# PEER stage: routing, weighing and the u-projection as one software pipeline with a kept order, and one of four one-hot products moved to ScalarE

## The chip, the cores and the metric

The kernel runs on one core of a Trainium2 chip. The metric is device time in microseconds (us) of one execution; a figure for a kernel is the median of its runs. One profiled execution gives the trace from which all rows here come. Engines carry the trace's names: PE is TensorE (PEld its weight loads), DVE VectorE, ACT ScalarE, POOL GpSimd, SP the engine that issues the loads.

## The reference, cut to what matters

The network has two blocks of two layers each on 256 tokens of width 1024. The change lies in the feed-forward part of the first block (PEER), which is run once in each of its two layers:

```python
def peer_ffn(h, w_q, sub_keys, u, v):          # u, v: 16384 experts x 1024
    q = (xc @ w_q).reshape(-1, 8, 2, 64)        # 8 heads, two halves
    s = jnp.einsum('thpd,pkd->thpk', q, sub_keys)
    sv, si = lax.top_k(s, 16)                   # best 16 of 128 keys, each half
    cand = sv[:, :, 0, :, None] + sv[:, :, 1, None, :]
    cand_id = si[:, :, 0, :, None] * 128 + si[:, :, 1, None, :]
    cv, ci = lax.top_k(cand, 16)                # best 16 pairs
    eid = jnp.take_along_axis(cand_id, ci, -1)
    g = softmax(cv)
    a = gelu(jnp.einsum('td,thkd->thk', xc, u[eid]))
    return jnp.einsum('thk,thkd->td', g * a, v[eid])
...
mods = silu(c) @ ada_w + ada_b                  # 12 x 1024 numbers, six vectors per layer
x = x + g1 * mixer(modulate(rms_norm(x), sh1, sc1))
x = x + g2 * peer_ffn(modulate(rms_norm(x), sh2, sc2), ...)
```

## The kernel before, in words

The kernel does not gather experts. It computes gelu(x u) for all 16384 experts in 128 **units** of 128 experts (`up`, lines 664 to 678), multiplies them by a dense weight that is zero where an expert was not chosen, and then accumulates all 128 units against v (`down`, lines 680 to 684).

*A unit of u.* A unit is 128 x 1024 weights, half of a 1 MB load (line 138, SP; two buffers `w_raw`). Every product is made from three: the weights are split into a rounded part `w_hi` (line 155, ACT) and a remainder `w_lo` (line 146, DVE or POOL), three buffers each, and 24 matmuls (lines 183 to 185) give 128 experts by 256 tokens in PSUM. The letters of a pattern say which engine makes `w_lo`: "P" is POOL, "V" is DVE, "VP" takes them in turn. ACT's gelu writes the unit into its place in `ring` (line 673). For tokens whose weights are already in `ring`, it writes to a scratch tile `sq` (line 676) and DVE multiplies that into `ring` (line 677).

*Routing.* After the keys' scores (line 744), DVE finds the top 16 of 128 for 32 rows (`top`, lines 716 to 721: maximum, index, replace, maximum, index), builds 50 candidates (line 756), finds their top 16, turns positions into key numbers (`ra`, lines 771 to 785; `eq`, lines 795 to 803), and makes the softmax (ACT's exp, line 783, between gelus, so ACT loads its function table for it and again afterwards). PE turns the results by six transposes (lines 816 to 818).

*Weighing.* For a block of 4 tokens (64 blocks) DVE builds two one-hot tiles of 128 x 512 (line 826: first key; line 828: second key) and multiplies the second by the high and by the low part of the softmax (line 830, two products, G1 and G2). PE makes 8 matmuls of 128 x 128 from them (lines 833 and 835), which is the dense weight of 128 x 128 experts for 4 tokens. DVE multiplies it into the units that are already done (line 839), and ACT copies it into the places of the units still to come (line 841).

*What sets the order.* Instructions are recorded in the order of the program, which calls `up` some units at a time between the parts of the routing, and two units after every four blocks. A scheduler with a cost model then orders each engine's stream by its own priorities; nothing in this stage pins it. The remaining `ada` blocks (the columns of ada_w that are needed late: 56 loads of 512 KB, line 381 on SP, each followed by a DVE multiply-and-sum of 128 x 1024, line 356) stand in the program in the down stage of PEER, one after every second unit. The scheduler moves them ahead to wherever SP and DVE look free.

## Time and profile before

| | us |
|---|---|
| median of 3 runs (lowest to highest) | 3672.56 (3648.35 to 3685.4) |
| the profiled execution, its time | 3682.53 |
| the profiled execution, its span | 3680.7 |
| mean granted clock of TensorE | 0.955 |
| PEER of layer 0: units of u with routing and weighing | 238 to 777.6 |
| PEER of layer 0: units of v | 777.6 to 1142.3 |
| PEER of layer 1: units of u with routing and weighing | 1381.5 to 1909.5 |
| PEER of layer 1: units of v | 1909.5 to 2274.2 |

The first 238 us hold the start of `ada` and the mixer of layer 0, 1142 to 1381 us the mixer of layer 1; the rest after 2274 us is the second block. PE is busy 94% of the whole span, so what can be gained lies in the stretches in which it isn't. A mean over the span hides those: the views are read stage by stage.

### The profile page before, as it was taken

The page shows a single profiled execution, that of the slowest core. Times are in us where ns is not written, and L with a number is a line of the kernel's source. Part 1 is how long each engine was busy: PE and PEld are TensorE (multiplying, and loading weights), DVE is VectorE, ACT ScalarE, POOL GpSimd, SP SyncE. Part 2 cuts the span into 40 slices and gives each one's busy share as a digit, 9 for nine tenths or more (in the row PEclk, how much of TensorE's full clock was granted, in tenths as well). Part 3 has the DMA queues.
Part 4 walks back from the last instruction along what each step waited for, and adds up shares of the span by engine and source line. Part 5 has one row for each costly group of instructions (what it writes and reads, how often), then busy time and mean ns, then how long its engine had stood idle before and what let it go on. Part 6 is the DMA issues. An engine that isn't in the chain of part 4 may idle for free.

```text
span 3680.7 us, 64031 instructions
## 1 busy us (share of the span) xinstructions
PE 3474.1 (94%) x26071; PEld 3201.5 (87%) x26071; DVE 2485.7 (68%) x4491; ACT 1738.2 (47%) x2934; POOL 1155.0 (31%) x536
## 2 busy tenths in 40 slices
PE   5888898999999998798999999999999999999999
PEld 4578888999998668787999999997769999978799
DVE  7689899877777449699777677555735454656544
ACT  3243444444445444344444445444644454555543
POOL 3165001444444126100444444443024232311422
PEclk9699899999999889899999999999979999999999
DMA  7554523755555113422555555543224555433254
GB/s 264 193 201 166 185 91 134 248 186 184 184 184 189 58 47 127 149 87 86 183 184 183 185 184 194 184 176 137 81 80 162 184 182 180 170 115 115 91 184 149
DMA packets 85848, 576.62 MB, mean 157 GB/s; under 512 B 9855, under 2 KB 11248, under 8 KB 20016
## 3 DMA queue, kind: packets, MB, share of 16 engines
q1 hardware_dynamic: 82448, 567.35, 43.0%
q8 instruction: 204, 3.34, 0.4%
q0 software_dynamic: 1520, 3.30, 0.3%
q10 hardware_dynamic: 1584, 1.88, 0.2%
q14 instruction: 92, 0.75, 0.1%
HBM read 571.54 MB, written 1.34 MB: 156 GB/s over the span
## 4 chain that ended last, share of the span: by engine, by line
PE 76%; DVE 16%; DMA 3%; ACT 2%; issue 2%; POOL 0%; ACTq 0%; SPq 0%; DVEq 0%; POOLq 0%
PE acc L185 13%; PE acc L184 13%; PE acc L183 13%; PE mm L185 8%; PE mm L183 8%; PE mm L184 8%; DVE w_lo L146 3%; DMA ada<-ada 3%; DVE ada L356 1%; PE g L833 1%; PE g L835 1%; DVE ring L839 1%; ACT w_hi L155 1%; PE pv L441 1%; DVE ring L721 1%
## 5 line engine op out<-in xcount | busy, mean ns | idle before, releaser
L146 POOL TENSOR_TENSOR w_lo<-w_raw,w_hi 128x1024 fp32r<-128x1024 f32 x441 | 1084.4, 2462 | 2450.9 <-ACT w_hi L155 2421.1
L155 ACT ACTIVATE w_hi<-w_raw 128x1024 fp32r<-128x1024 f32 x980 | 1037.8, 1060 | 1376.7 <-PE acc L184 676.3
L146 DVE TENSOR_TENSOR w_lo<-w_raw,w_hi 128x1024 fp32r<-128x1024 f32 x539 | 663.9, 1233 | 184.4 <-ACT w_hi L155 173.9
L183 PE MATMUL mm<-xh,w_hi 128*128 128x256 f32 (+1 forms) x2568 | 734.3, 287 | 18.8 <-ACT xh L316 11.1
L185 PE MATMUL mm<-xh,w_lo 128*128 128x256 f32 (+1 forms) x2568 | 738.0, 288 | 13.9 <-DVE w_lo L146 12.0
L184 PE MATMUL mm<-xl,w_hi 128*128 128x256 f32 (+1 forms) x2568 | 736.1, 287 | 4.6 <-DVE xl L317 3.0
L183 PE MATMUL acc<-wh,w_hi 128*128 128x256 f32 x2048 | 575.1, 281 | 0.0
L184 PE MATMUL acc<-wl,w_hi 128*128 128x256 f32 x2048 | 575.1, 281 | 0.0
L185 PE MATMUL acc<-wh,w_lo 128*128 128x256 f32 x2048 | 575.1, 281 | 0.0
L183 PEld LDWEIGHTS mm<-xh,w_hi 128*128 128x128 f32 (+1 forms) x2568 | 491.4, 192 | 33.2 <-issue 17.9
L185 PE MATMUL acc<-xh,w_lo 128*128 128x256 f32 (+1 forms) x1536 | 452.8, 295 | 68.7 <-DVE w_lo L146 65.7
L185 PEld LDWEIGHTS mm<-xh,w_lo 128*128 128x128 f32 (+1 forms) x2568 | 493.0, 192 | 23.0 <-DVE w_lo L146 17.3
L184 PEld LDWEIGHTS mm<-xl,w_hi 128*128 128x128 f32 (+1 forms) x2568 | 491.4, 191 | 13.5 <-issue 4.4
L446 DVE TENSOR_TENSOR wl<-ring,wh 128x256 fp32r<-128x256 f32 x256 | 359.5, 1405 | 185.2 <-ACT wh L445 185.1
L183 PE MATMUL acc<-xh,w_hi 128*128 128x256 f32 (+1 forms) x1536 | 446.1, 292 | 28.4 <-ACT xh L316 22.4
L184 PE MATMUL acc<-xl,w_hi 128*128 128x256 f32 (+1 forms) x1536 | 448.3, 292 | 3.4 <-DVE xl L270 2.7
L184 PEld LDWEIGHTS acc<-wl,w_hi 128*128 128x128 f32 x2048 | 386.3, 189 | 0.0
L183 PEld LDWEIGHTS acc<-wh,w_hi 128*128 128x128 f32 x2048 | 386.3, 189 | 0.0
L185 PEld LDWEIGHTS acc<-wh,w_lo 128*128 128x128 f32 x2048 | 386.3, 189 | 0.0
L185 PEld LDWEIGHTS acc<-xh,w_lo 128*128 128x128 f32 x1536 | 302.9, 197 | 78.3 <-DVE w_lo L146 74.2
L183 PEld LDWEIGHTS acc<-xh,w_hi 128*128 128x128 f32 x1536 | 301.6, 197 | 32.1 <-ACT xh L316 23.8
L184 PEld LDWEIGHTS acc<-xl,w_hi 128*128 128x128 f32 x1536 | 301.3, 196 | 6.6 <-DVE xl L270 3.9
(450 smaller groups left out, 6058.7 us busy)
## 6 DMA issues: line engine op xcount, KB each, us to landing
w_raw<-ffn SPq DMA_DIRECT2D x132, 1024.0 KB, 4.8
w_raw<-peer_u SPq DMA_DIRECT2D x128, 1024.0 KB, 4.8
w_raw<-peer_v SPq DMA_DIRECT2D x128, 1024.0 KB, 4.8
w_raw<-mix_in SPq DMA_DIRECT2D x48, 1024.0 KB, 4.8
ada<-ada SPq DMA_DIRECT2D x56, 512.0 KB, 4.2
w_raw<-mix_out SPq DMA_DIRECT2D x16, 1024.0 KB, 4.8
w_raw<-even_in SPq DMA_DIRECT2D x12, 1024.0 KB, 4.8
w_raw<-ada SPq DMA_DIRECT2D x12, 1024.0 KB, 4.8
```

The source lines that it names most:

```text
L146: ins = e.tensor_tensor(out, a, hi, op=OP.subtract)
L155: self.nc.scalar.activation(hi[:, :n], src, AF.Copy)
L183: mm(ps, wh, xh, start=start, stop=False, skip_group_check=True)
L184: mm(ps, wh, xl, start=False, stop=False, skip_group_check=True)
L185: mm(ps, wl, xh, start=False, stop=stop, skip_group_check=True)
L356: self.nc.vector.scalar_tensor_tensor(t, t, 1.0, self.silc, op0=OP.mult, op1=OP.mult, accum_out=self.mods[:, b:b + 1])
L441: mm(pv[o:o + 64, :], vrow[0], pts[:, 0:256], start=True, stop=False, skip_group_check=True)
L446: self.nc.vector.tensor_tensor(yl, src, yh.bitcast(F32), op=OP.subtract)
L721: nc.vector.max_index(idx[:, 8:16], vals[:, 8:16], r)
L833: nc.tensor.matmul(ps[:, t], oi[:, :, t], o[1][:, :, t], start=t == 0, stop=False, skip_group_check=True)
L835: nc.tensor.matmul(ps[:, t], oi[:, :, t], o[2][:, :, t], start=False, stop=t == TB - 1, skip_group_check=True)
L839: nc.vector.scalar_tensor_tensor(av[:, :, :n], ps[:, :, :n], 2.0 ** -15, av[:, :, :n], op0=OP.mult, op1=OP.mult)
```

## The change

Three things change. (1) Routing and weighing become a generator of small pieces, each with a DVE cost written beside it. One unit of u is made, then pieces are drawn up to a budget (2.6 us after a unit whose `w_lo` is POOL's, 1.55 us after one whose `w_lo` is DVE's). Splits of the weights are made three units ahead, the matmuls of a block come one unit later than its one-hot tiles, and the order in which this is written is pinned on PE, DVE and ACT for the whole stretch (`in_order`). Tops are made two rows at a time. The 64 blocks are spread over the units from about the 46th to the 126th. (2) Of the four one-hot products of a block, the low part (`o2`) is made by ACT: four activations of 128 x 128 with a scale for each partition, which write every fourth element. ACT's copy for the units to come now stands ahead of DVE's multiplication for the units done. (3) An `ada` load is tied to the load of v before it, and its DVE work to the down unit before it, so that all 56 lie in the down stage of layer 0. Of the `w_lo`, 30 per layer move from POOL to DVE.

```diff
+    @contextmanager
+    def in_order(self, *engines):
+
+        bb = self.nc.cur_bb
+        start = len(bb.bb.instructions)
+        yield
+        assert self.nc.cur_bb is bb
+        last = {}
+        for i in bb.bb.instructions[start:]:
+            if i.engine in engines:
+                if i.engine in last:
+                    self.tc.add_manual_dep(i, last[i.engine], mybir.DependencyInfo(
+                        mybir.DependencyClass.NoSync, mybir.DependencyReason.DATA), reason="in_order")
+                last[i.engine] = i.name
...
+        self.loaded = self.nc.sync.dma_start(t[:p, :n], src).ins
...
-    def ada_single(self, pool):
-
-        if self.ada_left:
+    def ada_singles(self, pool, after):
+
+        while self.ada_left:
+            k = len(ADA) - len(self.ada_left)
             b = self.ada_left.pop(0)
-            k = len(ADA) - len(self.ada_left) - 1
             t = pool.tile([128, D], F32, name="ada")
-            self.nc.sync.dma_start(t, self.io["ada"][k // 2, :, k % 2 * D:k % 2 * D + D])
-            self.ada_block(b, t)
+            with self.tc.issue_after(self.loaded):
+                self.nc.sync.dma_start(t, self.io["ada"][k // 2, :, k % 2 * D:k % 2 * D + D])
+            yield
+            with self.tc.issue_after(after()):
+                self.ada_block(b, t)
...
-        def up(n=1, pattern="P"):
-
+        ahead, later, waits, evacs = deque(), deque(), [], []
+
+        def keep():
+            for f in waits:
+                f()
+            waits.clear()
+
+        def up(pattern):
+
+            j, w = E.ups, E.weighed
+            E.ups += 1
+            ps = next(bank)
+            E.gemm(ps, ahead.popleft())
+            while later and later[0][0] < j:
+                later.popleft()[1]()
+            if w < T:
+                nc.scalar.activation(ring[:, j, w:], ps[:, w:], AF.Gelu_apprx_tanh)
+            if w:
+                t = E.nrm.tile([128, T], F32, name="sq", bufs=4)
+                nc.scalar.activation(t[:, :w], ps[:, :w], AF.Gelu_apprx_tanh)
             E.pattern, E.nlo = pattern, 0
-            for _ in range(n):
-                j, w = E.ups, E.weighed
-                E.ups += 1
-                ps = next(bank)
-                E.gemm(ps, next(ui))
-                if w < T:
-                    g = nc.scalar.activation(ring[:, j, w:], ps[:, w:], AF.Gelu_apprx_tanh)
-                if w:
-                    t = E.nrm.tile([128, T], F32, name="sq", bufs=4)
-                    g = nc.scalar.activation(t[:, :w], ps[:, :w], AF.Gelu_apprx_tanh)
-                    nc.vector.tensor_tensor(ring[:, j, :w], ring[:, j, :w], t[:, :w], op=OP.mult)
-            return g.ins
+            ahead.extend(islice(ui, 1))
+            keep()
+            if w:
+                nc.vector.tensor_tensor(ring[:, j, :w], ring[:, j, :w], t[:, :w], op=OP.mult)
...
             wh = V.tile([128, T], F32R, name="wh")
             wl = V.tile([128, T], F32R, name="wl")
-            E.parts(wh, wl, ring[:, j])
+            E.parted = E.parts(wh, wl, ring[:, j])
             E.accum(acc, next(vi), wh, wl, j == 0, j == NJ - 1)
 
...
+        def tops(rows, n):
+
+            v = nc.vector
+            rows = [row + (s2[:, k, :n],) for k, row in enumerate(rows)]
+            for vals, idx, src, r in rows:
+                v.max(vals[:, 0:8], src)
+            for vals, idx, src, r in rows:
...
+        def routing():
+
+            vector, scalar = nc.vector, nc.scalar
...
+                for tt in range(2):
+                    tops([(sv[:, tt, h, p], si[:, tt, h, p], s[:, tt, h, p]) for p in range(2)], 128)
+                    yield 2.4, "P" if h < 7 else "V"
...
+            for h in range(8):
+                tops([(cv[:, tt, h], ci[:, tt, h], cand[:, tt * 8 + h]) for tt in range(2)], 50)
+                yield 1.6, "P" if h < 5 else "V"
...
+            scalar.activation(ex, ex, AF.Exp)
...
+                        sl = slice(hf * 64, hf * 64 + 64)
+                        vector.tensor_tensor(eq[:, sl],
+                                             ra[:, p, tt * 128 + hf * 64:tt * 128 + hf * 64 + 64, None]
+                                             .to_broadcast([128, 64, 16]),
+                                             iota[:, None, 0:16].to_broadcast([128, 64, 16]), op=OP.is_equal)
+                        yield 1.2, "V"
...
+            yield None
+
+            def weigh(t0, oi, o1, o2):
+                def products():
+                    ps = g2.tile([128, TB, 128], F32, name="g2")
+                    for t in range(TB):
+                        nc.tensor.matmul(ps[:, t], oi[:, :, t], o1[:, :, t], start=t == 0, stop=False,
+                                         skip_group_check=True)
+                        nc.tensor.matmul(ps[:, t], oi[:, :, t], o2[:, :, t], start=False, stop=t == TB - 1,
+                                         skip_group_check=True)
+
+
+                    av = ring[:, :, t0:t0 + TB].rearrange("p j t -> p t j")
+                    n = E.ups
+
+                    def wait():
+                        if n < NJ:
+                            scalar.activation(av[:, :, n:], ps[:, :, n:], AF.Copy, scale=2.0 ** -15)
+
+                    def weights():
+                        vector.scalar_tensor_tensor(av[:, :, :n], ps[:, :, :n], 2.0 ** -15, av[:, :, :n],
+                                                    op0=OP.mult, op1=OP.mult)
+                        E.weighed = t0 + TB
+                    waits.append(wait)
+                    evacs.append(weights)
+                return products
...
+            for t0 in range(0, T, TB):
+                row = lambda g: g[:, None, t0:t0 + TB].to_broadcast([128, 128, TB])
+                oi = V.tile([128, 128, TB], BF, name="wh")
+                oj = E.nrm.tile([128, 128, TB], F16, name="sum", bufs=2)
+                o1 = V.tile([128, 128, TB], F16, name="wl")
+                o2 = E.nrm.tile([128, 128, TB], F16, name="sq", bufs=4)
+                vector.tensor_tensor(oj, row(JT), cols, op=OP.is_equal)
+                vector.tensor_tensor(oi, row(IT), cols, op=OP.is_equal)
+                vector.tensor_tensor(o1, oj, row(G1), op=OP.mult)
+
+                def rest(t0=t0, oj=oj, o2=o2):
+                    for t in range(TB):
+                        scalar.activation(o2[:, :, t], oj[:, :, t], AF.Copy, scale=G2[:, t0 + t:t0 + t + 1])
+                waits.append(rest)
+                later.append((E.ups, weigh(t0, oi, o1, o2)))
+                E.begun = t0 + TB
+                yield 0.5, "V"
+
+        pieces, due, pattern, weighing = routing(), 0.0, "P", 0
+
+        def settle():
+
+            for f in evacs:
+                f()
+            evacs.clear()
+
+        with E.in_order(*(e.engine for e in (nc.tensor, nc.vector, nc.scalar))):
+            E.pattern, E.nlo = pattern, 0
+            ahead.extend(islice(ui, 3))
+            while E.ups < NJ:
+                up(pattern)
+                settle()
+
+                due = min(due, 0.0) + (2.6 if pattern == "P" else 1.55)
+                while due > 0:
+                    if weighing and E.begun * (NJ - 2 - weighing) >= (E.ups - weighing) * T:
+                        break
+                    piece = next(pieces, None)
+                    if piece is None:
+                        break
+                    us, pattern = piece
+                    due -= us
+                    if E.begun and not weighing:
+                        weighing = E.ups - 1
+            for _ in chain(pieces, [None]):
+                keep()
+                while later:
+                    later.popleft()[1]()
+                    keep()
+                    settle()
...
+        blocks = E.ada_singles(A, lambda: E.parted)
         for j in range(NJ):
             down(j)
             if j % 2:
-                E.ada_single(A)
+                next(blocks, None)
```

**Order on ScalarE, weighing in layer 0.** Names: `ring<-g` is the copy of a block's weights into units to come, `ring<-mm` or `ring<-acc` and `sq<-...` the two pieces of a gelu, `w_hi` a split, `sq<-sum,g` the new products (line 914). Before:

```order
L155 ACTIVATE w_hi<-w_raw 128x1024
L673 ACTIVATE ring<-mm 128x224
L676 ACTIVATE sq<-mm 128x32
L673 ACTIVATE ring<-mm 128x224
L676 ACTIVATE sq<-mm 128x32
L155 ACTIVATE w_hi<-w_raw 128x1024
L841 ACTIVATE ring<-g_4062 128x4x82
L841 ACTIVATE ring<-g_4081 128x4x82
L155 ACTIVATE w_hi<-w_raw 128x1024
L673 ACTIVATE ring<-acc_1789 128x208
L841 ACTIVATE ring<-g_4100 128x4x82
L676 ACTIVATE sq<-acc_1789 128x48
```

After:

```order
L914 ACTIVATE sq<-sum,g_3866 128x128 x4
L892 ACTIVATE ring<-g_4489 128x4x70
L699 ACTIVATE ring<-acc_1789 128x220
L702 ACTIVATE sq<-acc_1789 128x36
L171 ACTIVATE w_hi<-w_raw 128x1024
L914 ACTIVATE sq<-sum,g_3866 128x128 x4
L892 ACTIVATE ring<-g_4545 128x4x69
L699 ACTIVATE ring<-acc_1790 128x216
L702 ACTIVATE sq<-acc_1790 128x40
L171 ACTIVATE w_hi<-w_raw 128x1024
```

Before, several blocks' copies stood in a row and splits came at irregular distances. Now each round holds one block's products, the copy of the block before it, one gelu and one split.

**Order on VectorE, weighing in layer 0.** `sum` and `wh` are the one-hot tiles, `sq<-sum` (before) and `wl<-sum` (after) products, `ring<-g,ring` the multiplication into units done. Before:

```order
L830 TENSOR_TENSOR sq<-sum,rs_r_3755 128x512 x4
L828 TENSOR_TENSOR sum<-rs_v_3754,cols 128x512
L839 SCALAR_TENSOR_TENSOR ring<-g_5060,ring 128x4x60
L839 SCALAR_TENSOR_TENSOR ring<-g_5079,ring 128x4x60
L830 TENSOR_TENSOR sq<-sum,rs_r_3755 128x512 x2
L826 TENSOR_TENSOR wh<-rs_v_3754,cols 128x512
L828 TENSOR_TENSOR sum<-rs_v_3754,cols 128x512
L146 TENSOR_TENSOR w_lo<-w_raw,w_hi 128x1024
L839 SCALAR_TENSOR_TENSOR ring<-g_5098,ring 128x4x60
L830 TENSOR_TENSOR sq<-sum,rs_r_3755 128x512 x2
L826 TENSOR_TENSOR wh<-rs_v_3754,cols 128x512
L828 TENSOR_TENSOR sum<-rs_v_3754,cols 128x512
```

After:

```order
L908 TENSOR_TENSOR sum<-rs_v_3864,cols 128x512
L909 TENSOR_TENSOR wh<-rs_v_3864,cols 128x512
L910 TENSOR_TENSOR wl<-sum,rs_r_3865 128x512
L162 TENSOR_TENSOR w_lo<-w_raw,w_hi 128x1024
L707 TENSOR_TENSOR ring<-ring,sq 128x64
L908 TENSOR_TENSOR sum<-rs_v_3864,cols 128x512
L909 TENSOR_TENSOR wh<-rs_v_3864,cols 128x512
L910 TENSOR_TENSOR wl<-sum,rs_r_3865 128x512
L162 TENSOR_TENSOR w_lo<-w_raw,w_hi 128x1024
L707 TENSOR_TENSOR ring<-ring,sq 128x64
L895 SCALAR_TENSOR_TENSOR ring<-g_4997,ring 128x4x68
```

Before, four blocks' work stood between two pairs of units. Now one block stands between two splits, with one product in place of two.

**Order of the loads on SP.** `peer_wq`, `peer_u` and `peer_v` are 1 MB each, `ada` 512 KB. Before, from the last loads of the mixer's end on:

```order
L138 DMA w_raw<-peer_wq 128x2048
L381 DMA ada<-ada 128x1024
L138 DMA w_raw<-peer_wq 128x2048
L381 DMA ada<-ada 128x1024
L138 DMA w_raw<-peer_u 128x2048
L381 DMA ada<-ada 128x1024
L138 DMA w_raw<-peer_u 128x2048
L381 DMA ada<-ada 128x1024
```

After:

```order
L154 DMA w_raw<-peer_wq 128x2048 x4
L154 DMA w_raw<-peer_u 128x2048 x64
L154 DMA w_raw<-peer_v 128x2048
L398 DMA ada<-ada 128x1024
L154 DMA w_raw<-peer_v 128x2048 x3
L398 DMA ada<-ada 128x1024
L154 DMA w_raw<-peer_v 128x2048
L398 DMA ada<-ada 128x1024
```

Before, `ada` alternated with the loads of wq and u; now no `ada` load stands among them, and it alternates with those of v.

## Rows read from the trace of the kernel before

**Rows 1.** Page, busy us of each engine, share of the span, instructions

```profile
PE 3474.1 (94%) x26071; PEld 3201.5 (87%) x26071; DVE 2485.7 (68%) x4491; ACT 1738.2 (47%) x2934; POOL 1155.0 (31%) x536
```

**Rows 2.** Windows: length, then PE, PEld, DVE, ACT, POOL busy, PE clock, DMA share

```profile
286.30:429.00 142.70, 117.74 (x915) 115.74 (x914) 128.66 (x370) 52.87 (x80) 43.49 (x18) 0.92 0.56 198
429.00:616.00 187.00, 164.50 (x1256) 149.97 (x1255) 170.42 (x385) 85.04 (x155) 0.00 (x0) 0.96 0.25 89
616.00:777.60 161.60, 159.99 (x1330) 159.78 (x1330) 132.31 (x122) 74.38 (x114) 71.99 (x28) 0.99 0.65 232
777.60:1142.30 364.70, 364.70 (x3074) 364.53 (x3072) 255.41 (x197) 175.78 (x258) 154.31 (x66) 1.00 0.52 186
...
286.30:777.60 491.30, 442.23 (x3496) 425.49 (x3495) 431.38 (x877) 212.29 (x349) 115.48 (x46) 0.96 0.47 168
1429.90:1909.50 479.60, 435.50 (x3497) 420.86 (x3496) 388.21 (x757) 213.01 (x348) 110.73 (x46) 0.96 0.38 137
```

**Rows 3.** Waits, 286.3 to 777.6 us: us in total, times, longest

```profile
ACT w_hi L155 <- DMA w_raw<-peer_u: 82.2, 34, 14.1
...
ACT ring L841 <- DVE ring L839: 75.1, 50, 3.3
...
PE acc L185 <- DVE w_lo L146: 32.0, 16, 9.4
...
DVE ada L356 <- DMA ada<-ada: 21.8, 17, 4.2
...
PE g L833 <- DVE sq L830: 5.3, 9, 1.7
```

**Rows 4.** Waits, 1429.9 to 1909.5 us

```profile
PE acc L185 <- DVE w_lo L146: 33.7, 14, 15.3
```

**Rows 5.** Timeline of PE in the weighing: start, us, instruction

```profile
600.33 0.29 PE L835 MATMUL g<-sq,wh 128*128 128x128 f16 x1
...
601.03 0.29 PE L835 MATMUL g<-sq,wh 128*128 128x128 f16 x1
```

**Rows 6.** Windows, a stretch of layer 1 (columns of rows 2)

```profile
1432.00:1462.00 30.00, 30.00 (x254) 30.00 (x253) 29.07 (x144) 13.83 (x21) 25.51 (x11) 1.00 0.53 189
```

**Rows 7.** Lines of DVE by form, 430 to 616 us: count, busy us, mean ns, idle

```profile
L830 DVE TENSOR_TENSOR sq<-sum,rs_r 128x512 f16<-128x512 f16 x128 | 48.1, 417 | 0.3 <-PE g L833 0.3
L146 DVE TENSOR_TENSOR w_lo<-w_raw,w_hi 128x1024 fp32r<-128x1024 f32 x30 | 36.5, 1217 | 0.0
...
L839 DVE SCALAR_TENSOR_TENSOR ring<-g,ring 128x256 f32<-128x256 f32 x4 | 3.0, 742 | 0.5 <-PE g L835 0.4
...
L677 DVE TENSOR_TENSOR ring<-ring,sq 128x144 f32<-128x144 f32 x2 | 0.6, 303 | 0.1
```

**Rows 8.** Lines of ACT by form, 430 to 616 us

```profile
L841 ACT ACTIVATE ring<-g 128x344 f32<-128x344 f32 x4 | 3.2, 793 | 5.9 <-DVE ring L839 5.9
...
L841 ACT ACTIVATE ring<-g 128x232 f32<-128x232 f32 x4 | 2.3, 586 | 5.0 <-DVE ring L839 4.9
```

**Rows 9.** Lines of ACT by form, 2560 to 2660 us

```profile
L433 ACT ACTIVATE p<-p,sm 128x128 f32<-128x128 f32 x16 | 6.4, 398 | 1.5 <-DVE sm L428 1.4
```

**Rows 10.** Timeline of ACT in the weighing

```profile
601.54 1.06 ACT L155 ACTIVATE w_hi<-w_raw 128x1024 fp32r<-128x1024 f32 x1 [1.37 <-PE acc L184]
602.50 0.17 ACT L673 ACTIVATE ring<-acc 128x16 f32<-128x16 f32 x1
...
603.16 0.41 ACT L676 ACTIVATE sq<-acc 128x240 f32<-128x240 f32 x1
```

**Rows 11.** Timeline of SP, loads of u

```profile
622.47 0.33 SPq L138 DMA_DIRECT2D w_raw<-peer_u  x1
...
710.04 51.54 SPq L138 DMA_DIRECT2D w_raw<-peer_u  x10
```

**Rows 12.** Chain that ended last, 150 to 238 us, by line

```profile
by line: DMA ada<-ada 23.7%; issue 11.5%; DVE ada L356 10.4%; DVE cv L557 7.8%; DVE cv L554 5.3%; DVE w_lo L146 4.0%; PE mm L183 3.8%; PE mm L185 3.7%; DVE x L408 3.6%; DVE xl L270 3.6%; ACT w_hi L155 3.4%; POOL w_lo L146 3.2%; PE mm L184 3
```

**Rows 13.** Lines of ACT by form, 286.3 to 430 us

```profile
L783 ACT ACT_TABLE_LOAD x1 | 1.3, 1283 | 0.0
```

More of the change, by code (lines that the diff above doesn't have):

```diff
@@ L1 @@
-from contextlib import ExitStack
-from itertools import chain
+from collections import deque
+from contextlib import ExitStack, contextmanager
+from itertools import chain, islice
 import numpy as np
@@ L709, in peer @@
         ra = take([2, 256], BF)
-        step, s2 = take([256], BF), E.nrm.tile([128, 1, 128], F32, name="rs_v256")[:, 0]
+        step, s2 = take([256], BF), E.nrm.tile([128, 2, 128], F32, name="rs_v256")
         ssum = E.nrm.tile([128, 16], F32, name="ssum")
```

181 lines of the change are left out of this document (78 added, 103 removed).

## The prediction

> **What bounds the kernel now.** I read the table of busy time by stage first. The page gives PE 94% of the span [rows 1], a mean that says little: in the v stage of layer 0 PE is busy for 364.70 of 364.7 us at clock 1.00, and in the last part of the u stage nearly as much, but at 286 to 429 us it is busy for 117.74 of 142.7 and at 429 to 616, where the weighing lies, for 164.50 of 187.0 [rows 2]. The granted clock falls to 0.92 and 0.96 there. In that weighing stretch DVE is busy for 170.42 of 187.0 us and POOL not at all: DVE is the bound. The whole stretch takes 491.3 us in layer 0 and 479.6 in layer 1, with 3496 and 3497 matmuls [rows 2].
>
> The list of waits says what PE stood for [rows 3]: `w_lo` from DVE (32.0 us, up to 9.4 at once), since routing work stood ahead of a split in DVE's queue; ACT waits for loads of u (82.2 us) because the two buffers of the load are freed by that same late split; and ACT's copy waits for DVE's multiplication (75.1 us in 50 waits). In layer 1 one wait of 15.3 us is nearly half of the 33.7 [rows 4]. So the idle time is an order on DVE, not a lack of it over the whole stretch: DVE is busy for 431.38 of 491.3 us in layer 0, and 388.21 of 479.6 in layer 1.
>
> **The change, part by part.** *What PE needs.* The pace without waits is 3074 matmuls in 364.7 us, 0.1186 each [rows 2], so a unit of 24 takes 2.85. A one-hot matmul starts every (601.03 - 600.33) / 6 = 0.117 us [rows 5], so a block of 8 takes 0.94. Of the 3496 in layer 0, 512 are one-hot and 6 transposes; 2978 x 0.1186 + 518 x 0.117 = 413.8 us. If PE never waits, the stretch shrinks by 491.3 - 413.8 = 77.5 us; layer 1 by 479.6 - 413.9 = 65.7. Together **-143**, which is the ceiling of the pipeline.
>
> *Does anything else set the round?* In the weighing a round with a block is 2.85 + 0.94 = 3.79 us of PE. DVE needs three one-hot operations at 0.417, a split at 1.217, a multiplication of the unit at about 0.30 and of the block at about 0.74 [rows 7]: 3.51, under 3.79, where before there were four one-hot operations and two units for four blocks. All `w_lo` of these rounds are DVE's, so POOL is off its back. ACT needs a split (1.06), two gelu pieces (0.17 + 0.41) [rows 10], a copy (0.59 at 128x232, 0.79 at 128x344 [rows 8]; with about 80 to 2 units left to copy, at most 0.75, half of it on average) and the four new activations. Their nearest row is another per-partition scaling of 128x128 on ACT, 0.398 [rows 9]. Back to back ACT instructions overlap: the split of 1.06 starts at 601.54 and the next instruction at 602.50 [rows 10], 0.10 less. So each costs 0.30, and ACT's round is 0.96 + 0.5 + 0.4 + 1.2 = 3.1 in the mean and 3.4 at the first blocks. It stays under PE's. The new activations write every fourth element, which that row doesn't; the copy of line 841, whose destination steps 1 KB, costs (793 - 586) / 112 = 1.85 ns an element [rows 8] against (1060 - 398) / 896 = 0.74 between the two contiguous ones. At that slope an activation is 0.54, four 2.16, and ACT's round 4.0. I take 0.30, since operation, shape and memory are those of rows 9, and keep 0.54 for the range: (4.0 - 3.79) x 128 = 27 us.
>
> The Trainium skill ("SBUF — State Buffer", Door 1) says that SBUF has 16-byte cachelines and that two hits in a line suffice for full bandwidth; a step of 8 bytes has two, so by that rule the four cost the 1.2 and nothing is added, and by the slope of line 841 the sum would be 27 worse. No run here shows such a step yet.
>
> The trace speaks against the move in one way: the product took DVE 0.417 [rows 7], and ACT is to take 1.2 to 1.6 for it [rows 9]. The Trainium skill ("ScalarE: Activation LUTs", Rules for kernel authors) says the same, to multiply on VectorE and not on ScalarE. By that rule the product stays, and DVE's round is 3.51 + 0.42 = 3.93, 0.14 over PE's, 18 us over 128 blocks; by the rows the move pays because ACT has the time.
>
> *Routing.* After a unit with POOL's split two tops of 128 are drawn, after one with DVE's at most 1.55 us of small operations, which with the split of 1.22 makes 2.77, under 2.85. Where the scheduler happened to mix them so, PE lost nothing: at 1432 to 1462 us DVE is 29.07 of 30 us busy, POOL 25.51, and PE 30.00 [rows 6]. The 30 splits per layer that move to DVE cost it 30 x 1.22 = 37 us, inside these rounds. If that cover went (a piece longer than its budget) `w_lo` would be late; being made three units ahead, it has two units, 5.7 us, of slack.
>
> *New waits.* The order is now fixed, so one late instruction holds its engine: exp brings a table load of 1.28 us [rows 13] and another back to gelu, in front of two gelus and splits; the turn of the results by PE waits for the whole `eq` chain; the first units have splits ahead only from the routing's start. Behind ACT's copy, which waits for PE's matmuls, stand a gelu and a split. None is seen before. Bounds: nothing (the splits are ahead), and half of all products waiting 0.59, which is what each of the 9 waits of 5.3 us was for a product [rows 3]: 64 x 0.59 = 38 plus some 10 at the two turns, near 50. I take the clean stretch [rows 6] as the nearer, but not as the whole: some 27 of the 128 products wait (16) and each turn costs 2, **+20**.
>
> *The ada loads.* 56 loads and their DVE work (1.2 us each) move into the v stage of layer 0, one per pair of units. SP alternates 1 MB and 512 KB. It did that before: from 622.47 to 710.04 us 15 loads of u with an ada between each took 5.84 us apiece, then 9 without took (51.54 - 0.33) / 9 = 5.69 [rows 11]. The added 0.15 x 56 is **+8** (0 to 72, if each costs the 21.8 / 17 = 1.28 us that DVE waited for a load [rows 3]). POOL, DVE and ACT had the same work per pair there, with a gelu and a multiplication where v has a copy and a subtraction.
>
> *The early stretch.* 20 of those loads leave the mixer of layer 0. Its chain from 150 to 238 us, 88 us, has the ada loads with 23.7% and their DVE work with 10.4% [rows 12], 20.9 and 9.2 us. The 1 MB loads that remain take the place in the queue, so I take DVE's part only: **-9** (0 to -30). The others leave the u stage, where they are already in the -143.
>
> Sum: -143 + 20 + 8 - 9 = **-124**. Against the profiled execution, 3682.53, that is 3558.5; it lies 10 us above the median of the runs shown, 3672.56, which gives 3548.6. I say **3550**.
>
> **The rivals.**
> - *The v stage pays the loads back.* There PE has no idle time at all, so anything that is late costs. For it: DVE's order puts the ada work between two subtractions and the split, so a late load holds the split. Against: rows 11. With 1.28 us for each, 72 instead of 8: **3614**.
> - *ACT or DVE sets the round by a little.* DVE's 3.51 and ACT's 3.4 are close to 3.79, and a fixed order turns jitter into waits. If each of 128 products waits 0.59 [rows 3], 75 us in place of 16 of the 20: **3609**. Up to 0.9 if the stride also counts: 3649.
> - *ACT becomes a closed loop, slower.* If the copy's wait for the matmuls of one block stands ahead of the activations that the matmuls of the next block need, the round is the sum 0.94 + 0.60 + 0.58 + 1.06 + 2.16 = 5.34 us with no overlap, 1.55 over PE's; 128 x 1.55 = 198, less 16: **3732**. It decides from 124 / 128 = 0.97 us per product on for no gain, and from 1.26 on for slower by over 1%. Against: in the order the activations of a block stand ahead of the copy of the block before, and its matmuls come a unit later.
> - *Nothing happens.* The 82.2 us that ACT waits for loads would be the loads' own. Then the idle time only moves: about **3665**. Against: the DMA share is 0.25 while PE idles, and 0.52 where PE is full [rows 2].
>
> **How the numbers follow.** Chances: forecast 0.67, loads paid back 0.13, round set by ACT or DVE 0.10, closed loop 0.05, nothing 0.05. The forecast's own range is 3515 (early stretch -30, new waits at about 7) to 3600 (new waits 50, loads some 25). With the first two rivals at 3609 and 3614 the range is **3515 to 3615**; the rest, and the tails, are left out. About 1%, 37 us, is what a measurement of this kernel can tell from no change, so faster means under 3636: 0.67 of the forecast, nearly all of the first rival and most of the second, 0.87; within 1%: 0.08; slower, the closed loop: 0.05.
>
> **What would show it.** In the table by stage the u stages of both layers are near 425 us with PE full at clock 1.00; DVE's and ACT's busy time in them near 90% of the span and neither with a repeated wait. The new activation near 0.40 us, not 0.54. ACT's waits for the loads of u gone. The v stage of layer 0 near 373 us, that of layer 1 unchanged at 364.7; the mixer of layer 0 about 9 us shorter. I am wrong if PE waits in each round for `sq` or `w_lo`, if the v stage of layer 0 passes 400 us, or if the u stage keeps a gap of more than 20 us at the turn from routing to weighing.

## The result and the profile after

The changed kernel takes 3554.53 us (median of 4 runs, 3541.91 to 3573.93) against 3661.56 before (4 runs, 3648.35 to 3685.4): a ratio of 0.9705, 95% interval 0.9631 to 0.978. The forecast was 3550, within 3515 to 3615. The profiled execution took 3541.91 us with a span of 3539.8.

Each trace is cut here at four kinds of marks: the first maximum of a routing, the first and the last matmul of a v stage, and the end. Lengths in us, from one profiled execution each:

| kernel | early | u, layer 0 | v, layer 0 | mixer, layer 1 | u, layer 1 | v, layer 1 | rest |
|---|---|---|---|---|---|---|---|
| before | 260.8 | 516.8 | 364.7 | 259.5 | 507.6 | 364.7 | 1406.6 |
| before, second trace (e1) | 258.8 | 524.8 | 364.7 | 259.5 | 507.7 | 364.7 | 1406.5 |
| changed | 248.3 | 443.2 | 393.1 | 239.6 | 447.9 | 361.1 | 1406.5 |
| changed, second trace (e9) | 246.8 | 441.9 | 394.2 | 244.6 | 448.0 | 369.2 | 1392.2 |

The change's own stages (early, both u, v of layer 0) give 12.5 + 73.6 + 59.7 - 28.4 = 117.4 us of the 140.9 between the first two spans. The other 23.5 are nearly all the mixer of layer 1, of which more under e1. The u stage of layer 0 before differs by 8 us between its two traces, so a difference of that size in one stage of one trace isn't read.

The first view is the windows of the changed kernel's stages; the columns are those of [rows 2], to whose stretches they answer: routing and weighing of layer 0, its v stage, then routing, weighing and v stage of layer 1.

```profile
248.30:400.00 151.70, 151.49 (x1259) 149.36 (x1260) 120.52 (x498) 77.56 (x125) 50.35 (x21) 0.99 0.48 174
400.00:687.00 287.00, 287.00 (x2414) 283.49 (x2413) 234.31 (x410) 218.05 (x555) 0.00 (x0) 1.00 0.42 149
691.50:1084.60 393.10, 371.81 (x3072) 367.56 (x3072) 322.10 (x319) 176.35 (x261) 160.69 (x65) 0.99 0.69 245
1324.20:1481.00 156.80, 156.70 (x1263) 153.59 (x1264) 121.00 (x499) 78.06 (x126) 50.36 (x21) 0.96 0.48 168
1481.00:1767.70 286.70, 286.70 (x2411) 283.26 (x2410) 233.98 (x409) 217.91 (x554) 0.00 (x0) 1.00 0.42 148
1772.20:2133.20 361.00, 360.93 (x3072) 360.54 (x3072) 255.18 (x198) 176.31 (x259) 153.06 (x64) 1.00 0.53 187
```

In the weighing, where DVE was busy for 170.42 of 187.0 us and PE idled [rows 2], PE is now busy in every microsecond of 287.00 at clock 1.00, DVE for 234.31 and ACT for 218.05. The same 64 blocks now lie on 287 us and no longer on 187. What is slower stands in the third row: the v stage of layer 0 has PE busy for 371.81 of 393.10 us.

The whole u stages, cut at the same marks, layer 0 and layer 1, first of the kernel before and then of the changed one (columns as above):

```profile
260.80:777.60 516.80, 466.72 (x3692) 447.66 (x3692) 455.99 (x1027) 227.73 (x381) 132.00 (x52) 0.96 0.47 168
1401.80:1909.50 507.70, 463.35 (x3694) 446.36 (x3695) 416.27 (x947) 228.02 (x379) 126.39 (x52) 0.96 0.38 135
```

```profile
248.30:691.50 443.20, 441.33 (x3693) 435.48 (x3693) 358.47 (x910) 296.50 (x682) 52.75 (x22) 1.00 0.44 157
1324.20:1772.20 448.00, 446.24 (x3694) 439.48 (x3694) 358.65 (x910) 296.85 (x683) 52.76 (x22) 0.98 0.44 154
```

Next the waits of the changed kernel, first of its u stage of layer 0, then of its v stage of layer 0; columns as in [rows 3].

```profile
DVE w_lo L162 <- ACT w_hi L171: 67.6, 77, 20.3
...
PE acc L199 <- ACT wh L464: 1.7, 1, 1.7
ACT w_hi L171 <- DMA w_raw<-peer_u: 1.4, 2, 1.2
PE g L780 <- ACT ring L782: 1.2, 1, 1.2
```

```profile
ACT w_hi L171 <- DMA w_raw<-peer_v: 34.1, 15, 4.3
DVE ada L372 <- DMA ada<-ada: 29.4, 38, 2.5
...
PE acc L200 <- DVE wl L465: 21.2, 19, 2.2
```

In the u stage PE's wait for `w_lo` (32.0 us in [rows 3]) is gone from the list, and ACT's wait for the loads of u is 1.4 us where it was 82.2 [rows 3], so the loads of u themselves were not the limit; DVE now waits for its input, as an engine with room does. In the v stage PE waits for `wl`, the remainder of the activations.

The new activations are seen in the timeline of ACT in the weighing (start, duration, instruction), and in its lines there by form (count, busy us, mean ns of one, idle):

```profile
556.89 1.49 ACT L914 ACTIVATE sq<-sum,g 128x128 f16<-128x128 f16 x4
558.12 0.53 ACT L892 ACTIVATE ring<-g 128x148 f32<-128x148 f32 x1
```

```profile
L914 ACT ACTIVATE sq<-sum,g 128x128 f16<-128x128 f16 x253 | 94.5, 577 | 0.0
```

Four take 1.49 us from the first start to the last end, and the next instruction starts 1.23 us after the first of them (558.12 - 556.89): 0.31 each, against the 0.30 taken from [rows 9, 10]. One by itself is 0.577 us long and not 0.40: it is longer than the contiguous one of [rows 9], but the next starts 0.27 us before its end.

### The profile page after: what moved, and what is told of

Read it like the earlier page. It is cut to its first block, busy times and chain, and to the rows that moved or that the text cites. A ratio compares the mean times of both kernels' runs of the same rounds, so it can differ in the third digit from the quotient of the medians.

```text
span 3539.8 us, 64455 instructions
## 1 busy us (share of the span) xinstructions
PE 3410.4 (96%) x26071; PEld 3166.7 (89%) x26071; DVE 2367.1 (67%) x4419; ACT 1877.4 (53%) x3544; POOL 1000.6 (28%) x476
## 4 chain that ended last, share of the span: by engine, by line
PE 84%; DVE 8%; DMA 4%; issue 2%; ACT 2%; POOL 0%; DVEq 0%; SPq 0%; ACTq 0%; POOLq 0%
PE acc L200 14%; PE acc L201 13%; PE acc L199 13%; PE mm L199 9%; PE mm L200 9%; PE mm L201 9%; DMA ada<-ada 4%; PE g L881 2%; PE g L883 2%; DVE w_lo L162 1%; DVE wl L465 1%; DVE ada L372 1%; PE pv L460 1%; ACT w_hi L171 1%; PE at L357 1%
## 5 line engine op out<-in xcount | busy, mean ns | idle before, releaser
L162 POOL TENSOR_TENSOR w_lo<-w_raw,w_hi 128x1024 fp32r<-128x1024 f32 x381 | 930.3, 2443 | 2471.5 <-ACT w_hi L171 1715.0
L162 DVE TENSOR_TENSOR w_lo<-w_raw,w_hi 128x1024 fp32r<-128x1024 f32 x599 | 740.1, 1236 | 292.0 <-ACT w_hi L171 273.9
L201 PE MATMUL mm<-xh,w_lo 128*128 128x256 f32 (+1 forms) x2568 | 730.2, 285 | 1.2 <-DVE w_lo L162 1.2
L200 PEld LDWEIGHTS mm<-xl,w_hi 128*128 128x128 f32 (+1 forms) x2568 | 487.8, 190 | 11.7 <-DVE xl L286 4.2
L200 PE MATMUL acc<-xl,w_hi 128*128 128x256 f32 (+1 forms) x1536 | 438.1, 285 | 1.6 <-DVE xl L286 0.8
L201 PE MATMUL acc<-xh,w_lo 128*128 128x256 f32 (+1 forms) x1536 | 436.9, 285 | 0.1
L199 PEld LDWEIGHTS acc<-xh,w_hi 128*128 128x128 f32 x1536 | 294.4, 192 | 25.4 <-ACT xh L332 23.5
L200 PEld LDWEIGHTS acc<-xl,w_hi 128*128 128x128 f32 x1536 | 293.4, 191 | 5.2 <-DVE xl L286 1.9
L201 PEld LDWEIGHTS acc<-xh,w_lo 128*128 128x128 f32 x1536 | 294.4, 192 | 1.5 <-issue 0.4
```

What stands on the lines that cost most here:

```text
L162: ins = e.tensor_tensor(out, a, hi, op=OP.subtract)
L199: mm(ps, wh, xh, start=start, stop=False, skip_group_check=True)
L200: mm(ps, wh, xl, start=False, stop=False, skip_group_check=True)
L201: mm(ps, wl, xh, start=False, stop=stop, skip_group_check=True)
```

## The experiments

**e1, the kernel before once more.**

> The kernel before, unchanged, for a second trace of it. Of the 141 us between the two profiled executions, 20 lie in the mixer of layer 1 (259.5 us before, 239.6 after), where both kernels have the same 1289 matmuls in the same order. Theory: that is the clock of that execution (0.76 to 0.80 granted over 120 us of it), not the change; then this trace has a mixer of layer 1 of another length than 259.5, nearer 240, and its u stages are again near 517 and 508 us from the first top to the first matmul of v. Rival: the change frees the mixer of layer 1 of something; then this trace has 259 us there again, at the same clock.

One run of 3688.52 us, span 3686.7. The u stages are 524.8 and 507.7 us, 8 more and the same. The mixer of layer 1 is 259.5 us again, so the theory as it was put, that another trace would have another length, fell for this kernel. The rival isn't borne out either: the windows of the same part of that mixer, first of the kernel before, then of the changed kernel, show what differs.

```profile
1229.00:1253.00 24.00, 24.00 (x77) 14.85 (x76) 9.58 (x47) 11.32 (x33) 3.65 (x3) 0.52 0.07 30
```

```profile
1174.30:1181.00 6.70, 6.70 (x25) 4.06 (x26) 3.54 (x18) 2.73 (x12) 0.49 (x1) 0.52 0.00 0
1181.00:1200.00 19.00, 18.92 (x86) 10.15 (x87) 12.28 (x60) 11.23 (x40) 2.89 (x2) 0.99 0.16 56
```

At about the same place (522 and 535 of the mixer's 1289 matmuls) the granted clock falls to the lower of its two levels (1.2 GHz) in both; before it stays there for 24 us, after for under 7. Over all traces that mixer took 259.5, 259.5, 250.4 (e6) and 243.2 (e7) with the order of before, and 239.6 to 251.7 with the new one. The two overlap, and the length goes with the granted clock of the stretch: 0.87 for 259.5 us in both traces of before, 0.91 for 250.4 (e6), 0.94 for 243.2 (e7), 0.96 for 239.6. So no more is claimed than this: these 20 us are clock, and what decides how long it stays low wasn't found. The last part of the program does the same, 1405 to 1407 us in five traces at a clock of 0.97 and 1386 to 1394 in nine others at 0.98 to 0.99, with TensorE's instructions in one order. Medians of one kernel also move by some 20 us between two sets of runs (the changed kernel: 3554.53, and 3531.72 in e9), and its runs go with their mean granted clock: 3573.93 us at 0.960, 3523.78 at 0.978. Stages are therefore compared below.

**e2, the low product back on VectorE.**

```diff
-                def rest(t0=t0, oj=oj, o2=o2):
-                    for t in range(TB):
-                        scalar.activation(o2[:, :, t], oj[:, :, t], AF.Copy, scale=G2[:, t0 + t:t0 + t + 1])
-                waits.append(rest)
+                vector.tensor_tensor(o2, oj, row(G2), op=OP.mult)
```

> The changed kernel with the low product made by VectorE (one more 128x512 product per block) and no longer by ScalarE (four activations). Theory: TensorE sets the weighing rounds at 3.79 us and VectorE has room, since its 410 instructions of one weighing stretch are busy for 234 of 287 us: 64 x 0.42 = 27 us more makes 261 of 287, so the time stays within 0.3% of the changed kernel (3555, say 3545 to 3565) and the weighing at 287 us. Rival: the moved product is what makes TensorE the bound; VectorE's round is then about 3.9 us with its waits, 0.14 over TensorE's, and the time is 15 to 40 us longer (3570 to 3595).

3542.24 us, ratio 0.9685 (0.9641 to 0.9729): no difference from the changed kernel. The u stages take 444.7 and 449.4 us (443.2 and 447.9), and the weighing, as a window of this kernel, is the same:

```profile
400.00:687.00 287.00, 287.00 (x2414) 283.47 (x2413) 249.25 (x471) 133.66 (x299) 0.00 (x0) 1.00 0.42 149
```

DVE has room for the fourth product: 249.25 us. Its one-hot operations of 0.42 us start 0.33 us apart, as this timeline of the changed kernel shows, so its round is shorter than durations add up to.

```profile
552.63 0.42 DVE L908 TENSOR_TENSOR sum<-rs_v,cols 128x512 f16<-128x512 bf16 x1
552.96 0.42 DVE L909 TENSOR_TENSOR wh<-rs_v,cols 128x512 bf16<-128x512 bf16 x1
```

The moved product isn't what makes the weighing PE-bound. In the u stage of layer 1, which never had ada blocks, VectorE has here every product it had before and 30 remainders more, and the stage is 449.4 us long against 507.6.

**e3, the same order without the pins.**

```diff
-        with E.in_order(*(e.engine for e in (nc.tensor, nc.vector, nc.scalar))):
+        if True:
```

> The changed kernel written in the same order, without the pins on TensorE, VectorE and ScalarE. The scheduler then changes VectorE's order within a block only (the multiplication into the units done goes ahead of two of the three one-hot operations), as far as the listing shows. Theory: the written order is what matters and the pin adds little: 3545 to 3575. Rival: without the pin routing pieces slide ahead of splits again and TensorE waits for the remainder as before: u stages 20 us longer or more each, 3595 to 3660.

3582.35 us, ratio 0.9763 (0.9723 to 0.9803). The weighing stays full; the u stages take 471.9 and 466.9 us, 28.7 and 19.0 more. The loss is in the routing. Its window, and PE's long waits in it, with one of ACT:

```profile
249.50:400.00 150.50, 132.14 (x1007) 128.62 (x1008) 126.40 (x480) 62.71 (x102) 52.22 (x21) 0.89 0.39 140
```

```profile
PE acc L201 <- DVE w_lo L162: 10.9, 2, 7.6
ACT ring L809 <- DVE ring L808: 8.6, 1, 8.6
...
PE acc L199 <- ACT w_hi L171: 5.7, 1, 5.7
```

There the scheduler lets routing pieces pass the splits, as before: from 346 to 358 us DVE compares key numbers (lines 837 to 848) ahead of the remainder for which PE waits 7.6 us, and ACT's exp for the softmax (line 809) holds the splits behind it while it waits 8.6 us for DVE. So the theory held for the weighing and the rival for the routing. Most of the gain is in the written order, some 48 us in the pin.

**e4, two places for ada in the ring.** Units of `ring` that the v stage has used up hold the ada blocks, DVE works on one a pair after its load, and the first is loaded four pairs later.

```diff
-            t = pool.tile([128, D], F32, name="ada")
+            t = ring[:, m % 2 * 4:m % 2 * 4 + 4].rearrange("p j t -> p (j t)")
...
             yield
-            with self.tc.issue_after(after()):
-                self.ada_block(b, t)
+            if old is not None:
+                with self.tc.issue_after(after()):
+                    self.ada_block(*old)
+            old = b, t
```

> The changed kernel with the ada loads of layer 0's v stage in two places of the ring that units already used have left, each multiplied one pair later, and the first of them four pairs later. Theory: the v stage of layer 0 is 393 us long and not 361 because there is one ada buffer: load 4.8 us, multiply 1.2, and the next load only behind the next load of v make a cycle of about 6.1 us per pair against 5.7, 0.4 to 0.5 x 56 = 22 to 28 us. With two places VectorE doesn't wait for ada loads (29.4 us in the changed kernel) and the stage takes 361 to 370 us: 3525 to 3540 in all. Rival: VectorE is overfull there because its two-input operations stop while GpSimd makes a remainder (2.42 us instead of 0.42); then the waits of TensorE for the remainder of the activations stay and the stage takes 385 or more: 3545 to 3560.

3509.84 us, ratio 0.9586 (0.9543 to 0.9628); the v stage takes 369.1 us and the u stages what they take in the changed kernel. For the stage the theory held; the whole is 15 us under its 3525 to 3540, and in this trace the last part of the program, which the edit leaves alone, is 13 us shorter than in the changed kernel's first (1393.6 against 1406.5). The waits of that stage: DVE no longer waits for an ada load, and PE hardly for `wl`.

```profile
ACT w_hi L171 <- DMA w_raw<-peer_v: 45.0, 18, 4.2
DVE wl L473 <- ACT wh L472: 43.8, 57, 2.9
...
PE acc L200 <- DVE wl L473: 2.7, 2, 1.4
```

**e5, the pipeline with the ada blocks untied**, as the kernel before has them (`ada_single` in place of `ada_singles`).

> The changed kernel with its pipeline, but the 56 late ada blocks written as before, untied: by the listing the scheduler again puts 20 loads into the mixer of layer 0 and the rest among the loads of u. Theory: the tie itself gives little, its gain early is paid back in v: the early part is again near 259 us (+10), the v stage of layer 0 361 to 365 (-28), the u stage of layer 0 takes 36 ada blocks of 1.2 us on VectorE, 43 us of which half are hidden: 443 + 10 to 25. In all 3540 to 3575. Rival: without the tie the pinned order suffers, since each ada block waits for its load in front of pinned work: u stage of layer 0 at 490 us or more, 3590 to 3630.

3542.0 us, ratio 0.9667 (0.9625 to 0.9708), no difference from the changed kernel that a median shows. Early part 260.5, u stage 469.1, v stage 361.1: 12.2 and 25.9 longer, 32.0 shorter. The tie moves the cost of these blocks; the 6 us that it saves between these two traces are less than the length of a v stage varies by from trace to trace (e9).

**e6, the tie alone on the kernel before.**

> The kernel before with one part of the change alone: the late ada blocks tied to the v stage of layer 0. Theory: early part 248 (-11), v stage of layer 0 390 to 393 (+28), u stage of layer 0 shorter by what its 36 ada blocks cost the VectorE that is its bound, up to 43 us: 517 to 475-500; layer 1 unchanged at 508. In all 3625 to 3660 against 3662 to 3666 of before. Rival: most of the change's gain in layer 0 is the ada work leaving: u stage of layer 0 at 460 or less, 3600 to 3615.

3675.94 us (10 runs), ratio 1.0005 (0.9968 to 1.0043): nothing. Early part 249.7, v stage 394.7, near what was expected; but the u stage of layer 0 is 505.9 and not 475 to 500, 11 or 19 us shorter than in the two traces of before. It gets no shorter than layer 1's, 505.3, which never had ada blocks, although DVE has 41 us less work in it (415.18 us busy against 455.99). DVE's amount of work over the stage was not the main thing that made it long.

**e7, the low product on ScalarE alone, on the kernel before**, by the edit of e2 the other way round.

> The kernel before with one part of the change alone: the low product made by ScalarE. Theory: in the weighing stretch of 187 us VectorE is the bound (170 us busy), and 64 x 0.42 = 27 us leave it in each layer, so each u stage gets 15 to 27 us shorter: 3610 to 3635. Rival: the scheduler's order, not VectorE's work, sets these stretches, and ScalarE's four activations stand in front of splits: 3645 to 3680.

3639.93 us (10 runs), ratio 0.9906 (0.9871 to 0.9941). The u stages take 500.2 and 496.2, 16.6 and 11.4 shorter: the lower end of what was expected. In the old order, with four blocks' products between two pairs of units, the product on ACT is worth some 28 us; in the pipeline (e2) nothing. DVE is busy for 46 us less in the two stages, so some 60% of the work taken away shows in the time, in e6 a quarter to a half, and PE is full in neither (here for 465.48 of the 500.2 us of layer 0).

**e8, a pipeline one unit shorter**, on the kernel of e4:

```diff
+            keep()
             E.gemm(ps, ahead.popleft())
-            while later and later[0][0] < j:
+            while later and later[0][0] <= j:
```

> The kernel of e4 (ada in the ring) with a pipeline one unit shorter: a block's matmuls come right after the unit behind which its one-hot tiles are made, and ScalarE's copy of a block stands ahead of the four activations of the next. Theory: TensorE's next unit, 2.85 us, covers the chain copy 0.6, one-hot 0.4, four activations 1.2; no wait at the products: 3505 to 3525, the weighing at 287 us. Rival (the closed loop of the prediction): the copy's wait for TensorE ahead of the activations closes a loop over both engines, 0.3 to 1 us per block: 3550 to 3640.

3714.11 us, ratio 1.014 (1.009 to 1.0191): 204 us slower than e4, 1.4% slower than the kernel before. The u stages take 544.2 and 547.3. The edit also moves ACT's four activations from behind the unit's split to ahead of its gelu. This is a closed loop as in the prediction (3732 there), though through other instructions, so that its round of 5.35 us below equals the 5.34 of that sum by luck. The timelines of ACT, DVE and PE in one round (the bracket is the idle time before and what ended it):

```profile
554.59 1.50 ACT L923 ACTIVATE sq<-sum,g 128x128 f16<-128x128 f16 x4 [1.87 <-DVE sum L917]
555.82 0.38 ACT L708 ACTIVATE ring<-mm 128x148 f32<-128x148 f32 x1
556.11 0.23 ACT L711 ACTIVATE sq<-mm 128x108 f32<-128x108 f32 x1
556.25 1.04 ACT L171 ACTIVATE w_hi<-w_raw 128x1024 fp32r<-128x1024 f32 x1
...
559.94 1.49 ACT L923 ACTIVATE sq<-sum,g 128x128 f16<-128x128 f16 x4 [2.25 <-DVE sum L917]
```

```profile
557.33 1.23 DVE L162 TENSOR_TENSOR w_lo<-w_raw,w_hi 128x1024 fp32r<-128x1024 f32 x1 [2.16 <-ACT w_hi L171]
558.47 0.27 DVE L716 TENSOR_TENSOR ring<-ring,sq 128x108 f32<-128x108 f32 x1
558.65 0.87 DVE L904 SCALAR_TENSOR_TENSOR ring<-g,ring 128x324 f32<-128x324 f32 x1
559.43 0.42 DVE L917 TENSOR_TENSOR sum<-rs_v,cols 128x512 f16<-128x512 bf16 x1
```

```profile
555.23 0.28 PE L890 MATMUL g<-wl,wh 128*128 128x128 f16 x1 [1.07 <-DVE wl L919]
...
560.58 0.29 PE L890 MATMUL g<-wl,wh 128*128 128x128 f16 x1 [1.32 <-DVE wl L919]
```

ACT's activations (554.59) hold back its gelu (555.82), that the split (556.25), that DVE's remainder (557.33), and behind the remainder and two multiplications stands the one-hot tile (559.43) for which ACT's next activations wait (559.94). Round the loop, one engine idles while the other works: 559.94 - 554.59 = 5.35 us, against the 3.79 that the prediction gave a round, and PE waits 1.07 and 1.32 us. In the changed kernel the activations come after the split and for matmuls a unit later, so that the gelu waits for no one-hot tile. Which of the two changes of this edit closes the loop, the unit less or the activations ahead of the gelu, no run separates.

**e9, the changed kernel once more.**

> The changed kernel, unchanged, for a second trace and beside the two that follow. Theory: u stages of 443 and 448 us, v stage of layer 0 393 and early part 248 again, since they hang on order and buffers; the mixer of layer 1 and the second block may differ by up to 20 us with the clock that was granted. 3540 to 3570. Rival: the u stages differ by more than 5 us between two traces; then the pipeline has waits that come and go.

3531.72 us (3523.78 to 3539.08), ratio 0.9614 (0.9543 to 0.9685). Early, u, v, u as in the table above, within 1.5 us: the pipeline's stages are the same in each trace. The v stage of layer 1, which the change leaves as it was, is 8 us longer than in the first trace:

```profile
1775.50:2144.70 369.20, 369.13 (x3072) 368.74 (x3072) 255.53 (x198) 176.47 (x260) 153.36 (x64) 1.00 0.52 183
```

PE is busy in all of it at clock 1.00, as in the 361.00 us of the first trace and the 364.70 of the kernel before. Its matmuls start 120.0 ns apart in the mean in this trace, 117.3 in the first, 118.7 before; why wasn't found. Differences of v stages under 8 us are therefore not read below.

**e10, all remainders of that v stage on VectorE**, with the one ada buffer:

```diff
-        E.pattern, E.nlo = "VP", 0
+        E.pattern, E.nlo = "VP" if l else "V", 0
```

> The changed kernel with all remainders of the v stage of layer 0 made by VectorE, so that GpSimd never stops it there (one ada buffer as in the changed kernel). Theory: the one buffer's cycle (load 4.8, multiply 1.2, wait for its turn on SP) sets 6.1 us per pair whoever makes the remainder: the stage stays at 385 to 395, 3545 to 3565. Rival: VectorE's lateness behind GpSimd is what hurts; then it is 365 to 372 and the whole 3520 to 3540.

3513.85 us, ratio 0.9578 (0.9495 to 0.9661); the v stage takes 365.0 us. The theory that the buffer's cycle sets the stage fell. Its rows: the waits of that stage, and DVE's lines (count, busy us, mean ns, idle) first of the changed kernel and then of this one.

```profile
DVE ada L372 <- DMA ada<-ada: 75.4, 55, 3.5
...
PE acc L200 <- DVE wl L465: 2.7, 3, 1.4
```

```profile
L465 DVE TENSOR_TENSOR wl<-ring,wh 128x256 fp32r<-128x256 f32 x128 | 174.4, 1377 | 38.9 <-ACT wh L464 38.7
```

```profile
L465 DVE TENSOR_TENSOR wl<-ring,wh 128x256 fp32r<-128x256 f32 x128 | 53.3, 417 | 0.5 <-ACT wh L464 0.5
```

The stop itself, in a timeline of the changed kernel, GpSimd and then DVE:

```profile
799.64 2.40 POOL L162 TENSOR_TENSOR w_lo<-w_raw,w_hi 128x1024 fp32r<-128x1024 f32 x1 [4.36 <-ACT w_hi L171]
```

```profile
799.90 2.42 DVE L465 TENSOR_TENSOR wl<-ring,wh 128x256 fp32r<-128x256 f32 x1 [0.98 <-ACT wh L464]
...
804.53 0.41 DVE L465 TENSOR_TENSOR wl<-ring,wh 128x256 fp32r<-128x256 f32 x1
```

DVE waits 75.4 us for ada loads in e10, more than twice as much, and PE doesn't notice, because the subtraction of line 465 takes 0.417 us and not 1.377: in the changed kernel half of them are stopped while GpSimd makes a remainder. In the v stages before, the same subtractions took 1405 ns in the mean of both and PE never waited [rows 2]: there DVE had no ada block between them. So neither the one buffer (removed in e4) nor the stop (removed in e10) alone costs much; a DVE that loses 2 us per pair to GpSimd and then waits for a load is late with `wl`.

**e11, both.**

> The kernel of e4 (two ada places in the ring) with all remainders of that v stage made by VectorE. Theory: both limits gone, VectorE needs 2 x 1.22 + 2 x 0.42 + 1.3 = 4.6 of 5.7 us per pair: 361 to 366 us instead of 369, 3500 to 3515 in all, no difference that a median shows. Rival: with the remainders all on VectorE the split of a late load finds no second engine and the stage gets longer than 372.

3501.32 us (3491.02 to 3503.43), ratio 0.9532 (0.9461 to 0.9603), v stage 362.3: 30 us under the changed kernel's median of the same set (e9), and, as expected, hardly to be told from e4 by a median.

**e12, splits two units ahead and not three**, on e11 (`islice(ui, 2)` for `islice(ui, 3)`).

> The kernel of e11 with the splits of the weights made two units ahead of TensorE and not three. Theory: after a unit's last matmul a gelu (0.4), the rounded part (1.0) and VectorE's remainder (1.2) make 2.6 us, under the 2.85 of the one unit that is left as cover, so the weighing rounds stay at 3.79 and their stretch at 287 us; with GpSimd's remainder (2.4) it is 3.8, about 1 us over, in the 21 units of routing whose remainder is GpSimd's: each u stage 15 to 25 us longer, 456 to 466. Rival: the third unit of lead is only for safety: u stages within 3 us of 441 and 449. Other rival: in the weighing too VectorE reaches the remainder late behind one-hot work: 20 us or more longer there.

One run, 3522.97 us. The u stages take 453.9 and 461.1 us, 13.1 and 11.7 more than e11. Windows of the routing, first in e11, then here, and of the weighing here, and PE's waits for GpSimd's remainder:

```profile
245.50:400.00 154.50, 154.35 (x1293) 152.44 (x1294) 123.38 (x503) 81.17 (x132) 50.11 (x21) 1.00 0.50 177
```

```profile
249.00:400.00 151.00, 142.08 (x1149) 136.81 (x1149) 109.28 (x476) 68.94 (x110) 46.47 (x20) 1.00 0.45 158
400.00:690.00 290.00, 290.00 (x2439) 286.66 (x2439) 236.70 (x414) 217.13 (x546) 0.00 (x0) 1.00 0.42 148
```

```profile
PE acc L201 <- POOL w_lo L162: 3.7, 5, 0.8
...
PE mm L201 <- POOL w_lo L162: 3.0, 4, 0.8
```

The place is the one expected, the routing with GpSimd's remainders; the size is a little under it (0.6 us per unit and not 1). In the weighing two units of lead are enough.

## Why the prediction was right, and the step that was off

- *PE sets the pace of the u stage, -143 and +20 for new waits.* Right. -73.6 and -59.7, together -133.3 against -123. The new waits were sized too high: PE is busy for 441.33 of 443.20 and 446.24 of 448.00 us, and the lists of waits have none for the 128 products. The longest wait is the 1.7 us at the end of a u stage, where the unit's and the last block's multiplication on DVE stand ahead of the first copy for v. The rest of what is missing to -143 isn't a wait of PE; part of it is the granted clock, 0.98 over the stage of layer 1. That the order of DVE's work and not its amount was the main fault is shown by e2 (more work in layer 1, 58 us gained), e6 (41 us less work, 11 to 19 us gained) and e3 (the same work without the pin, 48 us lost). No run moves the 30 remainders from GpSimd to DVE alone. By [rows 2] 28 of GpSimd's remainders lay after 616 us, where PE was full, and none in the weighing, so their going alone would not have freed the weighing.
- *The product on ACT costs nothing, at 0.30 for each.* Right in the price, 0.31, but not in the way to it: the sign that was named, a duration near 0.40 and not 0.54, came out at 0.577, and an overlap of 0.27 in place of 0.10 made up for it. That is luck in part. The step of 8 bytes costs no rate: the next start comes 0.29 to 0.31 us later for the contiguous activations of [rows 9] and 0.30 in the median here. Of the Trainium skill's two rules that of "SBUF — State Buffer" (Door 1), two hits in a line for full bandwidth, agrees with this, at 1.23 us for four. The Trainium skill's rule of "ScalarE: Activation LUTs" (Rules for kernel authors), to multiply on VectorE, would have cost 18 us by the prediction's sum, since that added durations without their overlap; e2 shows that it costs nothing. In the pipeline the rule holds and the move is needless; in the old order (e7) the move against it gained 28 us.
- *The ada loads in v, +8.* This step failed in size: +28.4, a part of the way to the first rival's 72. The prediction took the price from the loads of u before [rows 11] because "POOL, DVE and ACT had the same work per pair there, with a gelu and a multiplication where v has a copy and a subtraction". The work is the same, but nobody waits for the multiplication (before, those of line 677 from 622 to 708 us took up to 2.6 us, and the trace has no engine waiting for one), whereas PE needs the subtraction's result for the same unit. The right row was the wait for it, and DVE's stop behind GpSimd; e4 and e10 show either remedy.
- *The early part, -9.* -12.5, and 12 to 14 in the traces of e5 and e9 against their counterparts. The terms of ada cancel, as e5 and e6 show.
- *Sum.* -124 forecast, -117.4 in the stages named, -107 between the medians. That 3554.53 lies so near 3550 is luck: the u stages gave 10 us more than forecast and the early part 3.5, while the loads cost 20 more; the median of four runs before is 11 us under that of the three shown; and medians move by 20 us with the clock (e1). Nor were DVE and ACT busy for near 90% of the u stages, as was said: 81 and 67% in layer 0. The second rival (a round set by ACT or DVE) has no row for it: 287.00 of 287.00. A closed loop is real and slower than before (e8), but runs through ACT's activations and DVE's one-hot tiles and not through the copy; a block's matmuls a unit later, with ACT's activations behind the split, keep it open.

## What to carry to other kernels

Where one engine has idle time while another's busy share is high, first ask what stands ahead of the awaited instruction in the other's queue: here VectorE's products and 30 more remainders in another order filled TensorE (e2), and less work in the old order did not (e6, e7). Write a software pipeline with a whole unit between a producer on a second engine and its consumer; one unit less, which also put the producer ahead of other work on its engine, cost 204 us. When side work moves into a full stage, price it by the operation there that the bound engine waits for, not by a stretch in which the same engines do work that nobody awaits.

## What the runs showed of the hardware

In one and the same order of TensorE's instructions, the granted clock stayed at its lower level for 24 us in one kernel's trace and under 7 in the other's (windows under e1); such stretches make up to 20 us in the mixer of layer 1 and 11 to 20 in the second block. At clock 1.00 and without a wait, 3072 matmuls of one v stage took 361.00, 364.70 and 369.20 us in three traces (e9). ScalarE's activations of 128x128 that read and write every fourth 16-bit element were 577 ns long but started 0.30 us apart, where contiguous ones of 398 ns started 0.29 to 0.31 apart. Two-input VectorE subtractions of 128x256 took 2.42 us while GpSimd made a remainder and 0.42 otherwise, and their mean fell from 1377 to 417 ns when GpSimd had none to make (e10).
